# Half of an output product moved from the last stage of a decoder layer into its attention stage

## The chip, the cores and the metric

The kernel runs on one core of one Trainium2 chip. A core has a matmul engine (PE, with a weight load of its own, PEld), a vector engine (DVE), a scalar engine (ACT), GpSimd (POOL) and SyncE (SP), which here issues all the transfers. The metric is the device time of one execution in microseconds (us). Before the change it is 2042.25 us, the median of three runs (2040.35 to 2043.14).

## The reference

One decoder layer for 2048 tokens of width 1024, in f32. Shortened to what matters here:

```python
n = rms_norm(h, norm_g)
dq, dk, dv, dgate, cq, ckv, kr, mgate = jnp.split(n @ w_in, offsets, axis=-1)
# differential attention: 4 heads, 2 softmax maps a head, keys of 64, values of 128, causal
sc = jnp.einsum('bqhmd,bkhmd->mbhqk', rope(dq), rope(dk)) * 64 ** -0.5
pr = softmax(where(mask, sc, -inf))
od = rms_norm((pr[0] - lam * pr[1]) @ dv, subln_g) * (1.0 - lam_init) * silu(dgate)
# latent attention: 8 heads, from low-rank queries, keys and values, causal
om = mla_attention(...) * silu(mgate)
h = h + concatenate([od, om], axis=-1) @ w_out          # 1024 x 1024: rows 0-511 for od, 512-1023 for om
h = h + (p @ w_ple) * sigmoid(h @ w_ple_gate)           # 256 x 1024 and 1024 x 1024
return rms_norm(h, final_norm_g)
```

The output product is a sum over two halves of w_out: the rows that meet the differential heads (od) and those that meet the latent heads (om). The embedding product p @ w_ple depends on inputs alone.

## The kernel before

It works in four stages, one after the other, with tokens in 16 blocks of 128. Every f32 product is made as three matmuls of fp32r operands that are split in a high and a low part (high by high, high by low, low by high), so a product of 1024 by 512 columns is 8 x 3 matmuls of 512 columns.

1. Projections (0 to about 716 us): n @ w_in and what follows from it up to both attentions. Queries, keys and values, the gates (`gate_s`), all go to DRAM. The rotated queries and keys of the differential heads are stored split, in `dq_s`.
2. Latent attention (about 716 to 1162 us), ordered by a planner that is not touched. Its output goes to `zm_s`.
3. Differential attention (about 1162 to 1577 us). `load_head` brings a head's keys, queries and values: for each map one slot of queries (high part on partitions 0 to 63, low part on 64 to 127) and two slots of keys (high part twice, low part twice). The work is written in tasks. `block(h, b)` makes the scores of 128 queries against all earlier keys, in units of up to 1024 keys, for two maps: `unit` has the matmuls (L870, L871), a causal mask added by a matmul (L873) and the maximum on DVE (L874); when all units of a map are there, `expo` makes the negated, scaled maximum (L880 or L882) and the exponential on ACT, with its sum (L885). `combine` weighs the second map by lambda and the quotient of the sums and adds it to the first: on POOL for the first 1024 keys where there are two units (L899, L900), on DVE for the last unit (L902). `weigh(h, g)` takes two blocks: transposes of the probabilities (`tpa`, L930), a copy by ACT (`ah`, L932 or L934), products with the values (`pod`, L942), two transposes at the end (L952), the norm and a store to `zd_s`. `load_out` brings w_out and splits it in 32 pieces, in the last head.
4. Final stage (about 1577 to 2040 us), block by block from the last: `load_mix` loads attention output (1024 wide), gate, x and p, POOL makes gate times output (L807), 8 transposes (`zt4`), the output product p1 (48 matmuls, L1053 to L1055), x added by DVE (L1088), the embedding product p3 (12 matmuls), 8 transposes of the sum (`ht4`), the gate product p2 (48 matmuls), sigmoid, product, sum and norm. Weights for p3 and p2 are loaded and split at its start (L1033 to L1035), those for p3 first. `split_ps` (L110, L111) makes the high part by an ACT copy and the low part by a DVE subtraction.

PSUM holds 8 banks. In the differential stage: three score tiles of two banks each, one bank for transposes (`ps_t`), one for the products with values (`ps_o`).

The order on each engine comes from two things. `merge` deals the tasks of two lists by their costs, `weigh` of one pair of blocks with `block` of the next ones. The order that results is the priority by which a list scheduler of the framework places the instructions; so the order on an engine differs from that of the code. Each engine does its instructions in that order and waits on semaphores for the others.

Of the kernel before, what the change touches and what calls it, by code (L numbers as in the profile page):

```python
# [18 lines left out]
P = 128  # L19
# [6 lines left out]
LAM_INIT = 0.2  # L26
TWO_PI = 6.283185307179586
# [10 lines left out]
WN = 6  # L38
# [5 lines left out]
DROP = 3  # L44
TAIL = 2

# [18 lines left out]
def tile_hymba(ctx, tc, a, out):  # L65
# [19 lines left out]
    zm_s = [scratch(f"zm_s{t}", [512, 512]) for t in range(NT)]  # L85

# [109 lines left out]
    with ExitStack() as c1:  # L196
# [162 lines left out]
        for m in range(2):  # L359
            wg, wn = wn, (load_w(512, 512) if m == 0 else load_w(2560, 272))  # L360
            for t in range(NT):
# [4 lines left out]
                for g in range(4):  # L366
# [8 lines left out]
                    V.tensor_mul(t1, pt, tcos)  # L375
                    for q in range(4):
                        V.tensor_mul(t2[32 * (q ^ 1):32 * (q ^ 1) + 32], pt[32 * q:32 * q + 32],
                                     tsin[32 * q:32 * q + 32])
# [218 lines left out]
    def load_head(h):  # L597

        ts = list(range(NT)) if h % 2 == 0 else list(reversed(range(NT)))
        hd = heads[h] = {}  # L600

        def begin():
            for t in ts:
                tg = dict(tag="vbig", bufs=2) if h % 2 == 1 and t >= 2 else dict(tag="big")
                hd[t] = xpool.tile([P, 7, 512], F32R, name="hd", **tg)

        def one(t, m, i):
            for j in range(2 + i * 2):
                nc.sync.dma_start(out=hd[t][64 * (j % 2):64 * (j % 2) + 64, 3 * m + i + j // 2].bitcast(F32),
                                  in_=dq_s[i][t][j // 2 if i == 1 else j, h, m * 64:(m + 1) * 64, :])  # L610

        def val(t):
            nc.sync.dma_start(out=hd[t][:, 6].bitcast(F32).rearrange("p (j d) -> p j d", d=P),
                              in_=dv_s[t][:, h * P:(h + 1) * P].rearrange("(j p) d -> p j d", p=P))

        tasks = [(0, begin)] + [(0.5, lambda t=t, m=m, i=i: one(t, m, i)) for m in range(2) for i in range(2) for t in ts]
        return tasks + [(0.1, lambda t=t: val(t)) for t in ts]

# [181 lines left out]
    def mix(b, zg, gt):  # L800

        t, o = b // 4, (b % 4) * P
        nc.sync.dma_start(out=zg[:, 0:512], in_=zd_s[b // 2][b % 2 * P:(b % 2 + 1) * P, :])
        nc.sync.dma_start(out=zg[:, 512:1024], in_=zm_s[t][o:o + P, :])
        nc.sync.dma_start(out=gt, in_=gate_s[b])
        for g in range(2):
            G.tensor_mul(zg[:, g * 512:(g + 1) * 512], zg[:, g * 512:(g + 1) * 512], gt[:, g * 512:(g + 1) * 512])  # L807


    SC_D = 64.0 ** -0.5  # L810
    with ExitStack() as c3:
# [12 lines left out]
        def load_out():  # L824

            tasks = []

            def piece(n):
                k, c = n // 4, n % 4
                if n % 8 == 0:  # L830
                    wt[k // 2] = xpool.tile([P, 2, 2, D], F32R, name="wo", tag="big")
                w = wt[k // 2]
                sl = slice(c * 256, (c + 1) * 256)
                ws = sb.tile([P, 256], F32, name="ws", tag="ws", bufs=3)
                nc.sync.dma_start(out=ws, in_=a["w_out"][k * P:(k + 1) * P, sl])
# [3 lines left out]
            return [(0.3, lambda n=n: piece(n)) for n in range(4 * KT)]  # L839
# [3 lines left out]
        ends = []  # L843

        def block(h, b):
# [8 lines left out]
            def unit(m, u):  # L854
                hd = heads[h]
                if m == 0 and u == 0:
                    st["s"] = sm.tile([P, 2, 2], F32, name="ssum", tag="ssum", bufs=4)
                if u == 0:
# [301 lines left out]
```

## Time and profile before

| | before |
|---|---|
| median of the runs (3) | 2042.25 us |
| profiled execution | 2042.74 us |
| its span, first to last instruction | 2040.5 us |
| mean granted clock of PE over the span | 0.982 |
| latent stage, differential stage, final stage | 446, 415, 463.5 us |

The profiled execution's own time is 2.2 us more than its span. A row of stretches gives start, end and length in us, then the busy time of an engine with its number of instructions in brackets, then PE's granted clock (1.00 is full speed), the DMA share and GB/s. A row of operations gives line, engine, operation, output and inputs, shapes and count, then busy us and the mean ns of one, then the engine's idle time just before them and what ended it. A row of the timeline gives start, duration and the same names; the numbers in square brackets are idle time before it.

### The profile page before, as it was taken

What the parts mean: (1) busy time and instruction counts of PE and PEld (TensorE: products, weight loads), DVE (VectorE), ACT (ScalarE), POOL (GpSimd) and SP (SyncE); (2) the same over time, 40 slices, a digit from 0 to 9 for tenths busy, and PEclk for the clock granted to TensorE, in tenths of its full rate; (3) what the DMA queues carried; (4) which work ended last, traced back from release to release, by engine and by line L of the source; (5) the groups of instructions that cost most, each with busy time, mean ns of one, the idle gap of its engine ahead of it and who ended that gap; (6) DMA issues with size and microseconds to landing.
All of it is one profiled execution on the core that took longest, in us unless ns stands there. A gap on an engine that the chain in (4) does not pass through costs nothing.

```text
span 2040.5 us, 28322 instructions
## 1 busy us (share of the span) xinstructions
PE 1930.3 (95%) x9521; PEld 1520.2 (74%) x9521; DVE 1208.1 (59%) x2685; ACT 917.7 (45%) x2089; POOL 634.4 (31%) x528
## 2 busy tenths in 40 slices
PE   7999999999999699999999989899988899999997
PEld 5788878898887477777777667676666677777786
DVE  5253677632446487888888687677876533333322
ACT  4422001122333467777777677677776311111111
POOL 4400345300000166666656335414441201111100
PEclk9999999999998899999999899999998999999999
DMA  5442333322267643514141311530021522222210
GB/s 165 140 147 87 130 127 135 119 86 77 65 211 255 219 127 105 144 55 130 31 118 42 101 35 43 154 112 27 24 83 56 194 90 68 88 88 88 75 47 21
DMA packets 171680, 209.73 MB, mean 103 GB/s; under 512 B 38876, under 2 KB 99180, under 8 KB 171536
## 3 DMA queue, kind: packets, MB, share of 16 engines
q1 hardware_dynamic: 171536, 207.93, 32.6%
q8 instruction: 75, 1.23, 0.3%
q14 instruction: 69, 0.57, 0.1%
HBM read 129.65 MB, written 78.14 MB: 102 GB/s over the span
## 4 chain that ended last, share of the span: by engine, by line
PE 75%; DVE 7%; ACT 7%; DMA 3%; POOL 2%; issue 2%; SPq 1%; ACTq 0%; POOLq 0%; DVEq 0%
PE p L1053 6%; PE p L1055 6%; PE p L1054 6%; PE ps L252 5%; PE ps L251 5%; PE ps L253 5%; PE pod L942 3%; PE pm L171 3%; PE po L704 3%; PE ps L372 3%; PE pst L675 3%; PE ps L370 3%; PE ps L371 3%; PE po L705 3%; PE pst L674 3%; PE pst L673 3%
## 5 line engine op out<-in xcount | busy, mean ns | idle before, releaser
L690 POOL TENSOR_TENSOR acc<-ph,acc 128x512 f32<-128x512 f32 (+3 forms) x208 | 216.6, 1041 | 165.2 <-DVE acc L685 76.2
L251 PE MATMUL ps<-wh,xh 128*128 128x512 f32 (+1 forms) x640 | 229.6, 359 | 9.6 <-DVE wh L240 7.9
L252 PE MATMUL ps<-wl,xh 128*128 128x512 f32 (+1 forms) x640 | 227.6, 356 | 0.5 <-DVE wl L241 0.4
L253 PE MATMUL ps<-wh,xl 128*128 128x512 f32 (+1 forms) x640 | 226.7, 356 | 0.4 <-DVE xl L228 0.3
L678 ACT ACTIVATE ph<-pst 128x512 fp32r<-128x512 f32 (+1 forms) x320 | 170.2, 532 | 114.1 <-PE pst L675 61.6
L695 DVE TENSOR_TENSOR pl<-pst,ph 128x512 fp32r<-128x512 f32 (+1 forms) x320 | 193.3, 607 | 45.7 <-ACT pst L679 42.9
L874 DVE TENSOR_REDUCE mxd<-pu 128x1 f32<-128x1024 f32 (+4 forms) x192 | 173.1, 908 | 61.9 <-PE pu L873 39.0
L885 ACT ACTIVATE pb<-pu,nm 128x1024 f32<-128x1024 f32 (+4 forms) x192 | 165.6, 866 | 39.3 <-DVE nm L880 25.7
L679 ACT ACTIVATE pst<-pst 128x512 f32<-128x512 f32 (+1 forms) x320 | 169.0, 528 | 0.0
L107 POOL TENSOR_TENSOR s<-s,half 128x2 f32<-128x2 f32 (+1 forms) x48 | 32.6, 679 | 425.0 <-DVE s L106 359.6
L870 PE MATMUL pu<-hd 128*128 128x512 f32 (+3 forms) x320 | 139.8, 437 | 20.6 <-ACT pb L885 17.6
L942 PE MATMUL pod<-ah,hd 128*128 128x256 f32 (+1 forms) x576 | 146.5, 379 | 0.5 <-ACT ah L934 0.5
L251 PEld LDWEIGHTS ps<-wh,xh 128*128 128x128 f32 x640 | 121.5, 190 | 30.2 <-ACT sq L223 6.6
L173 DVE TENSOR_REDUCE mx<-pm 128x1 f32<-128x512 f32 x192 | 130.0, 680 | 14.9 <-PE pm L171 14.8
L253 PEld LDWEIGHTS ps<-wh,xl 128*128 128x128 f32 x640 | 121.2, 190 | 20.1 <-DVE xl L228 2.7
L252 PEld LDWEIGHTS ps<-wl,xh 128*128 128x128 f32 x640 | 121.7, 190 | 18.9 <-DVE wl L241 1.8
L1102 DVE TENSOR_TENSOR sg<-p,sg 128x512 f32<-128x512 f32 (+1 forms) x34 | 20.8, 655 | 175.1 <-ACT sg L1101 175.1
L871 PE MATMUL pu<-hd 128*128 128x512 f32 (+3 forms) x320 | 122.6, 390 | 0.0
L704 PE MATMUL po<-ph,vall 128*128 128x512 f32 (+1 forms) x320 | 117.9, 374 | 4.8 <-ACT ph L678 4.5
L673 PE MATMUL pst<-QH,kall 97*128 97x512 f32 (+2 forms) x296 | 119.1, 402 | 0.0
L171 PE MATMUL pm<-kall,QH 96*128 96x512 f32 (+3 forms) x296 | 115.0, 403 | 3.6 <-DVE mx L173 2.5
L705 PE MATMUL po<-pl,vall 128*65 128x512 f32 (+1 forms) x320 | 115.4, 363 | 0.0
(265 smaller groups left out, 4735.1 us busy)
## 6 DMA issues: line engine op xcount, KB each, us to landing
hd<-dq_s SPq DMA_DIRECT2D x192, 128.0 KB
wr<-in_w_in SPq DMA_DIRECT2D x40, 256.0 KB
xr<-in_xT SPq DMA_DIRECT2D x32, 256.0 KB
dq_s<-th SPq DMA_DIRECT2D x32, 256.0 KB
dq_s<-tl SPq DMA_DIRECT2D x32, 256.0 KB
k_s<-stage SPq DMA_DIRECT2D x16, 512.0 KB
q_s<-stage SPq DMA_DIRECT2D x16, 512.0 KB
v_s<-stage SPq DMA_DIRECT2D x16, 512.0 KB
```

Of the source, the lines that this page charges most:

```text
L171: T.matmul(pm[:, :w], lhsT=q, rhs=keys_of(pr, e, c)[0][0:96, :w], start=True, stop=True)
L251: T.matmul(pt[:, :w], lhsT=h, rhs=wh[k][:, :w], start=(k == 0), stop=False)
L252: T.matmul(pt[:, :w], lhsT=h, rhs=wl[k][:, :w], start=False, stop=False)
L253: T.matmul(pt[:, :w], lhsT=l, rhs=wh[k][:, :w], start=False, stop=(k == KT - 1))
L673: T.matmul(pt[:, o:], lhsT=kh[0:97], rhs=qh[0:97, o:], start=True, stop=False)
L678: A.activation(ph[:, o:], pt[:, o:], AF.Exp, scale=SC_M)
L690: eng.tensor_add(self.acc[:, o:], ph[:, o:].bitcast(F32), self.acc[:, o:])
L695: V.tensor_sub(pl[:, o:], pt[:, o:], ph[:, o:].bitcast(F32))
L704: T.matmul(self.po[:, o:], lhsT=vv[:, 0:128], rhs=ph[:, o:], start=(kc == 0), stop=(kc == self.n - 1))
L705: T.matmul(self.po2[:65, o:], lhsT=vv[:, 64:129], rhs=pl[:, o:], start=(kc == 0), stop=False)
L874: V.reduce_max(st["x", m][:, u:u + 1], pu[:, :w], axis=AX.X)
L942: T.matmul(st["po"][:, o:], lhsT=vv, rhs=st[u][:, i, o:], start=(kc == 0), stop=(kc == nk - 1))
```

## The change

- A new task list, `side_work`, in the differential stage: for each block it loads x, the latent output, its half of the gate and p; POOL makes gate times output; four transposes (`tpf`) go to the transpose pool of that stage; ACT and DVE split them; 24 matmuls (`pf<-wm`) make the latent half of the output product, DVE adds x, and the sum goes to DRAM (`h_s`); 12 matmuls (`pf<-wp`) make the embedding product, copied by ACT and stored (`ple_s`). Both use one PSUM bank, `ps_f`. Its weights (`wm`, `wp`) are loaded and split at the start of the stage. The other half of w_out (`wd`) is loaded in the last 15% of the list (`TAIL_D`). `merge(main, fill)` deals it all among the attention's tasks.
- The final stage loads `h_s` and `ple_s`; it makes 4 transposes of the attention output, not 8, 24 matmuls of the output product, not 48, and no embedding product. The embedding weights are no longer loaded there.
- A head's keys are stored once, high part on partitions 0 to 63 and low part on 64 to 127; the queries, which then must be there twice, are loaded in groups of two blocks (`load_dq`) into two slots that take turns. The number of score matmuls is the same.
- The maximum is kept per unit: DVE makes the negated maximum of a unit, for the second unit the smaller of the two, and the exponential follows each unit (`step`, one unit later in priority). `combine` then corrects the first unit by exp of the difference of the two: a small ACT exponential, two small DVE products and one more POOL scaling of 1024 columns (L989) for each block with two units. The factor 1/8 of the scores goes into the queries in the first stage, by a form with a scalar in place of 160 multiplications.
- PSUM of the differential stage: two score tiles (were three), two banks for transposes (was one), one for values, one for `ps_f`.

The core of the diff:

```diff
@@ first stage @@
-                    V.tensor_mul(t1, pt, tcos)
+                    sc = SC_D if m == 0 else 1.0
+                    V.scalar_tensor_tensor(t1, pt, sc, tcos, op0=ALU.mult, op1=ALU.mult)
...
@@ load_head @@
+        def keys(t, i):
+            nc.sync.dma_start(out=hd[t][64 * i:64 * i + 64, 0:2].bitcast(F32),
+                              in_=dq_s[1][t][i, h].rearrange("(m p) s -> p m s", p=64))
...
+    def load_dq(h, g):
+        q, t, o = heads[h]["q", g % 2], g // 2, g % 2 * 256
+        for i in range(2):
+            for r in range(2):
+                nc.sync.dma_start(out=q[64 * r:64 * r + 64, :, i].bitcast(F32),
+                                  in_=dq_s[0][t][i, h, :, o:o + 256].rearrange("(m p) s -> p m s", p=64))
...
@@ differential stage @@
-        ps_s = c3.enter_context(tc.tile_pool(name="p3pss", bufs=3, space=PSUM, reuse_waits="tile"))
-        ps_t = c3.enter_context(tc.tile_pool(name="p3pst", bufs=1, space=PSUM, reuse_waits="tile"))
+        ps_s = c3.enter_context(tc.tile_pool(name="p3pss", bufs=2, space=PSUM, reuse_waits="tile"))
+        ps_t = c3.enter_context(tc.tile_pool(name="p3pst", bufs=2, space=PSUM, reuse_waits="tile"))
         ps_o = c3.enter_context(tc.tile_pool(name="p3pso", bufs=1, space=PSUM, reuse_waits="tile"))
+        ps_f = c3.enter_context(tc.tile_pool(name="p3psf", bufs=1, space=PSUM, reuse_waits="tile"))
...
+        def side_work(wk, wz, b):
...
+            def load():
+                nc.sync.dma_start(out=xr, in_=a["x"][b * P:(b + 1) * P, :])
+                mix(zm, gt, zm_s[b // 4][b % 4 * P:(b % 4 + 1) * P, :], b, 1)
+            def turn():
+                tp = ps_t.tile([P, 4, P], F32, name="tpf", tag="tpa")
+                for k in range(4):
+                    T.transpose(tp[:, k], zm[:, k * P:(k + 1) * P], ident)
+                split_ps(zh, zl, tp)
...
+            def mul(name, xs, kts, c, n0, n1, end):
...
+                if n0 == 0:
+                    box[0] = ps_f.tile([P, 512], F32, name="pf")
+                for n in range(n0, n1):
+                    T.matmul(box[0], lhsT=steps[n][0], rhs=steps[n][1][:, sl], start=(n == 0), stop=(n == len(steps) - 1))
+                if n1 == len(steps):
+                    end(sl)
+            def add(sl):
+                V.tensor_add(xr[:, sl], box[0], xr[:, sl])
+                if sl.start:
+                    nc.sync.dma_start(out=h_s[b], in_=xr)
+            def keep(sl):
+                A.copy(pe[:, sl], box[0])
...
-                V.reduce_max(st["x", m][:, u:u + 1], pu[:, :w], axis=AX.X)
-            def expo(m):
...
+                V.tensor_reduce(nm[:, m, u:u + 1], pu[:, :w], op=ALU.max, axis=AX.X, negate=True)
+                if u == 1:
+                    V.tensor_tensor(nm[:, m, 1:2], nm[:, m, 0:1], nm[:, m, 1:2], op=ALU.min)
+                def expo():
+                    A.activation(st[m][:, u * 1024:u * 1024 + w], pu[:, :w], AF.Exp, bias=nm[:, m, u:u + 1],
+                                 accum_out=st["s"][:, m, u:u + 1])
+                step([(1, expo)] + ([(2, combine)] if (m, u) == (1, nu - 1) else []))
...
+                if nu == 2:
+                    V.tensor_mul(f[:, 1:2], f[:, 1:2], cc)
+                    sl = slice(0, 1024)
+                    for m in range(2):
+                        G.tensor_scalar(st[m][:, sl], st[m][:, sl], scalar1=f[:, m:m + 1], scalar2=0.0, op0=ALU.mult,
+                                        op1=ALU.add)
+                    G.tensor_add(st[0][:, sl], st[0][:, sl], st[1][:, sl])
...
+        fill = [(0.3, f) for f in load_split_w("wm", a["w_out"], 4, 4, dict(tag="vbig", bufs=2))]
+        fill += [(0.3, f) for f in load_split_w("wp", a["w_ple"], 0, 2, {})]
+        fill += [x for b in range(NB) for x in side_work(wk, wz, b)]
+        wd = load_split_w("wd", a["w_out"], 0, 4, dict(tag="big"))
+        rest = sum(c for c, _ in fill) * TAIL_D / (1 - TAIL_D)
+        fill += [(rest / len(wd), f) for f in wd]
+        merge(main, fill)
...
@@ final stage @@
-        load_split(*wl, a["w_ple"], 2)
         load_split(*wg, a["w_gate"], KT)
...
-            product(p1, zh, zl, *wo, KT)
+            product(p1, zh, zl, *wo, 4)
...
-            p3 = ps.tile([P, D], F32, name="p3", tag="p4")
-            product(p3, ph, pl, *wl, 2)
```

On PE, the matmul engine, in the differential stage. `pu` is a score tile, `tpa` a transpose of probabilities, `pod` the product with values; x2 or x4 means so many in a row. Before, in the first head:

```order
L930 MATMUL tpa<-ident,pb 128x128 x4
L942 MATMUL pod<-ah,hd 128x256 x2
L873 LDWEIGHTS ident_b
L873 MATMUL pu<-mask_b,ident_b 128x128
L930 MATMUL tpa<-ident,pb 128x128 x4
L942 MATMUL pod<-ah,hd 128x256 x2
L870 MATMUL pu<-hd 128x512
L871 MATMUL pu<-hd 128x512
```

With the change, also in the first head. `tpf` is the transpose of the latent output, `pf` the side accumulator, `wm` the latent half of w_out:

```order
L1034 MATMUL pod<-ah,hd 128x256 x2
L882 MATMUL tpf<-ident,wk 128x128 x4
L1022 MATMUL tpa<-ident,pb 128x128 x4
L958 MATMUL pu<-hd 128x512
L959 MATMUL pu<-hd 128x512
L958 MATMUL pu<-hd 128x512
L959 MATMUL pu<-hd 128x512
L961 LDWEIGHTS ident_b
L961 MATMUL pu<-mask_b,ident_b 128x128
L899 MATMUL pf<-wm,wz 128x512 x4
L1034 MATMUL pod<-ah,hd 128x256 x2
L1022 MATMUL tpa<-ident,pb 128x128 x4
```

Between the attention's own matmuls, which keep their order, stand transposes and groups of four matmuls of the side work.

On PE in the final stage, at the end of one block's output product. `zg` is the next block's attention output, `xr` this block's sum, `ht4h` the transposed sum's high part, `wl` the embedding weights, `wg` the gate weights. Before:

```order
L1055 MATMUL p_17703<-wo,zt4l 128x512
L1045 MATMUL tp_17756<-ident,zg 128x128 x4
L1045 MATMUL tp_17763<-ident,zg 128x128 x4
L1053 MATMUL p_17770<-wl_16890,ph_17524 128x512
L1054 MATMUL p_17770<-wl_16892,ph_17524 128x512
...
L1054 MATMUL p_17770<-wl_16893,ph_17524 128x512
L1055 MATMUL p_17770<-wl_16891,pl_17525 128x512
L1045 MATMUL tp_17785<-ident,xr_17520 128x128 x4
L1045 MATMUL tp_17792<-ident,xr_17520 128x128 x4
L1053 MATMUL p_17799<-wg,ht4h 128x512
```

With the change:

```order
L1161 MATMUL p_18643<-wd,zt4l 128x512
L1151 MATMUL tp_18672<-ident,zg 128x128 x4
L1151 MATMUL tp_18681<-ident,xr_18514 128x128 x4
L1159 MATMUL p_18695<-wg,ht4h 128x512
L1151 MATMUL tp_18688<-ident,xr_18514 128x128 x4
L1160 MATMUL p_18695<-wg,ht4h 128x512
```

The twelve matmuls of the embedding product are gone from between the output product and the transposes of its sum, and the second four of those transposes stand behind the first matmul of the gate product.

## Rows read from the trace of the kernel before

**Rows 1.** Engines on the page: busy us, share of the span, instructions.

```profile
PE 1930.3 (95%) x9521; PEld 1520.2 (74%) x9521; DVE 1208.1 (59%) x2685; ACT 917.7 (45%) x2089; POOL 634.4 (31%) x528
```

**Rows 2.** Stretches: bounds, length, then PE, PEld, DVE, ACT, POOL, clock, DMA, GB/s.

```profile
1162.00:1577.00 415.00, 368.11 (x1952) 282.09 (x1952) 311.34 (x731) 301.14 (x780) 157.02 (x97) 0.97 0.23 67
716.00:1162.00 446.00, 438.26 (x2185) 322.41 (x2183) 367.80 (x823) 325.59 (x699) 275.86 (x255) 1.00 0.34 93
1650.00:1960.00 310.00, 306.71 (x1392) 246.00 (x1391) 105.13 (x168) 50.58 (x112) 36.28 (x34) 1.00 0.25 81
1240.00:1280.00 40.00, 36.97 (x197) 28.86 (x197) 29.79 (x57) 28.77 (x63) 20.20 (x11) 1.00 0.24 69
1460.00:1540.00 80.00, 64.76 (x333) 49.90 (x334) 63.75 (x123) 55.34 (x140) 37.85 (x21) 0.96 0.21 68
```

**Rows 3.** Timeline of PE in the differential stage.

```profile
1244.82 0.60 PE L930 MATMUL tpa<-ident,pb 128*128 128x128 f32 x4
1245.25 1.03 PE L942 MATMUL pod<-ah,hd 128*128 128x256 f32 x4
1246.12 0.22 PE L873 MATMUL pu<-mask_b,ident_b 128*128 128x128 bf16 x1
```

**Rows 4.** Timeline of PE in the final stage.

```profile
1828.14 0.40 PE L1053 MATMUL p<-wg,ht4h 128*128 128x512 f32 x1
1830.01 0.40 PE L1055 MATMUL p<-wg,ht4l 128*128 128x512 f32 x1
```

**Rows 5.** Score matmuls L870: idle before them until (us, times).

```profile
  ACT pb L885: 51.9, 90
```

**Rows 6.** Transposes L930: idle before them until (us, times).

```profile
  ACT ah L932: 48.4, 74
```

**Rows 7.** Chain that ended last, in the final stage.

```profile
1656.31 0.88 PE tp L1045 x8
1987.79 0.87 PE tp L1045 x8
```

**Rows 8.** Timeline at the final stage's start: SP's issues, a DVE split.

```profile
1584.12 1.75 SPq L1033 DMA_DIRECT2D wr<-in_w_ple  x4
1590.25 2.13 SPq L1033 DMA_DIRECT2D wr<-in_w_gate  x4
...
1616.38 1.35 DVE L1035 TENSOR_TENSOR wg<-wr,wg 128x512 fp32r<-128x512 f32 x2 [3.28 <-ACT wg L1034]
```

**Rows 9.** Operations of ACT: count, busy us and mean ns, idle before.

```profile
L885 ACT ACTIVATE pb<-pu,nm 128x1024 f32<-128x1024 f32 x80 | 89.2, 1116 | 27.8 <-DVE nm L880 25.7 <-DVE nm L882 1.3
L932 ACT COPY ah<-tpa 128x512 f32<-128x512 f32 x112 | 65.2, 582 | 20.6 <-PE tpa L930 17.0 <-PE pu L873 3.2 <-ACT pb L885 0.2
```

**Rows 10.** Timeline in the final stage: the weight load that waits.

```profile
1826.75 0.19 PEld L1053 LDWEIGHTS p<-wg,ht4h 128*128 128x128 f32 x1 [0.53 <-ACT ht4h L110]
```

**Rows 11.** Operations of DVE, same columns as rows 9.

```profile
L874 DVE TENSOR_REDUCE mxd<-pu 128x1 f32<-128x1024 f32 x80 | 97.5, 1219 | 34.9 <-PE pu L871 21.8 <-PE pu L873 12.4
L837 DVE TENSOR_TENSOR wo<-ws,wo 128x256 fp32r<-128x256 f32 x32 | 22.9, 734 | 3.1 <-ACT wo L836 3.1
L1088 DVE TENSOR_TENSOR xr<-p,xr 128x512 f32<-128x512 f32 x32 | 20.6, 686 | 61.7 <-PE p L1055 61.7
L891 DVE TENSOR_TENSOR ssum<-ssum 128x2 f32<-128x2 f32 x32 | 4.9, 154 | 8.7 <-ACT pb L885 8.7
L375 DVE TENSOR_TENSOR t<-ps,tcos 128x512 f32<-128x512 f32 x32 | 22.1, 692 | 52.5 <-PE ps L372 44.5 <-DMA tcos<-tab_s 6.5 <-issue 1.4
L228 DVE SCALAR_TENSOR_TENSOR xl<-xr,norm_g,xh 128x512 fp32r<-128x512 f32 x32 | 27.8, 872 | 44.1 <-ACT xh L220 44.0
```

**Rows 12.** Operations of POOL, same columns.

```profile
L899 POOL TENSOR_SCALAR pb<-pb,cc 128x1024 f32<-128x1024 f32 x32 | 54.2, 1693 | 98.0 <-DVE cc L895 45.3 <-DVE nm L880 33.7 <-ACT wo L836 6.0
L807 POOL TENSOR_TENSOR zg<-zg,gt 128x512 f32<-128x512 f32 x30 | 40.9, 1385 | 142.4 <-PE p L1055 81.0 <-DMA zg<-zd_s 28.4 <-DMA gt<-gate_s 23.8
```

**Rows 13.** DVE subtraction L1072: shortest, median and longest in ns.

```profile
L1072 DVE TENSOR_TENSOR pl<-pr,ph x16: 414/1360/1539, 1581.6 to 1991.6; 128x256 fp32r<-128x256 f32 x16
```

More of the change, by code (lines that the diff above doesn't have):

```diff
@@ L26 @@
 LAM_INIT = 0.2
+SC_D = 0.125
 TWO_PI = 6.283185307179586
@@ L44, with merged @@
 DROP = 3
+TAIL_D = 0.15
 TAIL = 2
+def merged(a, b):
+    out = []
+    merge(*([(x[0], lambda x=x: out.append(x)) for x in y] for y in (a, b)))
+    return out
 def merge(a, b):
@@ L85, in tile_hymba @@
     zm_s = [scratch(f"zm_s{t}", [512, 512]) for t in range(NT)]
+    h_s = [scratch(f"h_s{b}", [P, D]) for b in range(NB)]
+    ple_s = [scratch(f"ple_s{b}", [P, D]) for b in range(NB)]
     const = ctx.enter_context(tc.tile_pool(name="const", bufs=1))
@@ L798, in tile_hymba, with mix, zd_of @@
             tick()
[L800 to L810, printed above, removed]
+    def mix(zg, gt, src, b, c):
+        nc.sync.dma_start(out=zg, in_=src)
+        nc.sync.dma_start(out=gt, in_=gate_s[b][:, c * 512:(c + 1) * 512])
+        G.tensor_mul(zg, zg, gt)
+    def zd_of(b):
+        return zd_s[b // 2][b % 2 * P:(b % 2 + 1) * P, :]
     with ExitStack() as c3:
@@ L822, in tile_hymba, with load_split_w, piece @@
         wt = {}
[L824 to L832, printed above, removed]
+        def load_split_w(name, src, k0, kts, tg):
+            def piece(k, c):
+                if k % 2 == 0 and c == 0 and (name, k // 2) not in wt:
+                    wt[name, k // 2] = xpool.tile([P, 2, 2, D], F32R, name=name, **tg)
+                w = wt[name, k // 2]
@@ L843, in tile_hymba, with step @@
         ends = []
+        def step(new=()):
+            for x in late:
+                x[0] -= 1
+            due = [x for x in late if x[0] <= 0]
+            late[:] = [x for x in late if x[0] > 0] + [list(x) for x in new]
+            for _, f in due:
+                f()
         def block(h, b):
@@ L868, in unit @@
                     o = pu[:, c * 512:c * 512 + cw]
-                    q = hd[t][:, 3 * m, j * P:(j + 1) * P]
-                    T.matmul(o, lhsT=q, rhs=hd[kc][:, 3 * m + 1, :cw], start=True, stop=False)
-                    T.matmul(o, lhsT=q, rhs=hd[kc][:, 3 * m + 2, :cw], start=False, stop=not last)
+                    qh, ql = (hd["q", b // 2 % 2][:, m, i, b % 2 * P:(b % 2 + 1) * P] for i in range(2))
+                    T.matmul(o, lhsT=qh, rhs=hd[kc][:, m, :cw], start=True, stop=False)
@@ L945, in finish @@
             def finish():
+                while ends:
+                    ends.pop(0)()
                 ot = sb.tile([P, 256], F32, name="otd", tag="otd", bufs=1)
@@ L974, in weigh, with finish_late, next_end, last_mix @@
             return tasks
-        order = [(h, g if h % 2 == 0 else NB // 2 - 1 - g) for h in range(4) for g in range(NB // 2)]
+        order = [(h, g) for h in range(4) for g in groups(h)]
         blocks = [(h, 2 * g + j) for h, g in order for j in range(2)]
         LEAD = 3
-        for x in blocks[:LEAD]:
-            merge(block(*x), [])
-        pending, wload = [], load_out()
+        def finish_late():
+            while late:
+                step()
+        def next_end():
+            if ends:
+                ends.pop(0)()
+        def last_mix():
+            box["mixed"] = xpool.tile([P, 2, 512], F32, name="mixed", tag="vbig", bufs=2)
+            mix(box["mixed"][:, 0], box["mixed"][:, 1], zd_of(NB - 1), NB - 1, 0)
+        box = {}
+        main = [x for y in blocks[:LEAD] for x in block(*y)]
+        pending = load_head(1)
+        pending.pop(0)[1]()
+        wt["wp", 0] = xpool.tile([P, 2, 2, D], F32R, name="wp", tag="big")
+        wk = xpool.tile([P, 4096], F32, name="wk", tag="big")
+        wz = pp.tile([P, 1536], F32R, name="wz")
         for i, (h, g) in enumerate(order):
-            if i % 8 == 0 and h < 3:
+            if i % 8 == 0 and 0 < h < 3:
                 pending = load_head(h + 1)
-            if h == 3:
-                pending, wload = pending + wload[:WN], wload[WN:]
             n = -(-len(pending) // max(1, HE - i % 8)) if h < 3 else len(pending)
```

159 lines of the change are left out of this document (81 added, 78 removed).

## The prediction

> **What bounds the kernel now.** I read the page's engine table first: PE, the matmul engine, is busy 1930 of the 2040.5 us [rows 1]. Then the table of stretches, one row for each stage [rows 2]. In the latent stage (716 to 1162 us) PE is busy 438 of 446 us at full clock, in the middle of the final stage (1650 to 1960) 307 of 310. Those two do nothing but what PE needs. In the differential stage (1162 to 1577) it is busy 368 of 415, and DVE, ACT and POOL are further from full than that. So it is the only stage with room on PE, and the room is larger than the busy column says, because a matmul's record is longer than the time until the next may follow. I therefore read the spacing of starts on the timeline. Four transposes take 1245.25 − 1244.82 = 0.43 us, 0.108 each; two value products (each two records of 256 columns) take 1246.12 − 1245.25 = 0.87, 0.435 each [rows 3]. A 512-column matmul takes 0.234: eight intervals from 1828.14 to 1830.01 [rows 4].
>
> At these spacings the differential stage of before needs: scores, counted in the code, 4 heads x 2 maps x 34,816 columns, two passes folded in, 278,528 columns at 0.234 per 512 = 127 us; 288 value products at 0.43 = 124; 606 transposes at 0.108 = 65; 128 mask products at about 0.06, the 0.05 between its start and the next row's being a lower end and its own 0.22 an upper, = 8. That is 324 us of the 415: 91 us in which PE could have done more. The clock explains about 12 of them (mean granted clock 0.97 in this stage [rows 2], 415 x 0.03). Most of the rest is two waits: score matmuls wait 51.9 us until the exponential has freed a score tile [rows 5], transposes wait 48.4 us until ACT has emptied the one transpose tile [rows 6] (these lists count the weight-load queue with the matmul queue, so their sum may be over 91).
>
> **What moves.** Out of the final stage, for each of 16 blocks: 24 of the 48 matmuls of the output product, the 12 of the embedding product, and 4 of 16 transposes. 36 x 0.234 + 4 x 0.108 = 8.86 us a block, 141.8 in all. The same instructions come into the differential stage, so its floor becomes 324 + 142 = 466 us. Moving them gains nothing by itself: it pays only as far as they fall into PE's 91 us.
>
> **Final stage, given back.** In the steady part the chain of waits is PE alone: from the transposes at 1656.31 to those at 1987.79 lie 12 blocks, 27.62 us each, of which 8.86 go [rows 7]. Two things keep the stage from giving all 141.8. First, the gate weights. Now the embedding weights are asked for at 1584.12, the gate weights from 1590.25, and the last piece is split at 1616.38 + 1.35 = 1617.7 [rows 8]; until then PE lives on the output and embedding products of two blocks, some 15 us of which are gone. The gate weights are now first in the queue, 6.1 us earlier, so 15 − 6 = 9 us are lost. Second, the 12 embedding matmuls (2.8 us) stood between the output product and the transposes of its sum; without them ACT has two copies of 0.58 to make [rows 9] before the gate product may start, where before it had one. Such a wait shows already as 0.53 us [rows 10]; I take another 0.5 for about 14 blocks, 6 to 7 us (0 if the next block's work fills it, 16 if both the sum's 0.69 [rows 11] and a copy are uncovered). Sum: −141.8 + 9 + 6 = −127 us.
>
> **Differential stage.** Its other engines first, each new piece priced at its nearest row. DVE: 32 additions at 0.686, 16 splits of the same size, 8 more weight pieces at 0.734, and about 160 operations on one or two columns at 0.154 [rows 11]: 22 + 11 + 6 + 25 = 64, so at most 375 busy us. ACT: 16 + 32 copies at 0.582 [rows 9], 8 weight copies and 32 one-column exponentials, at most that again = 28 + 23: at most 352. POOL: 32 more scalings at 1.693 and 16 products at 1.385 [rows 12], 32 operations of half that size at most 1.385: 54 + 22 + 44 = 120, at most 277. All stay under the 466 of PE and near the proportions of the latent stage, where DVE has 368, ACT 326 and POOL 276 beside a PE busy 438 of 446 [rows 2]. So I expect no other engine to become the bound; POOL's second scaling is hidden as there, and if it were not, it would delay a block's transposes by 1.7 us, 32 times = 54 us.
>
> The waits. A pair of score tiles was freed late, because the exponential of the first 1024 keys had to wait for the maximum of the second: from the last score matmul of the first unit, one more unit of PE work (324 / 192 units = 1.7), a maximum of 1.22, a small operation of 0.15 and the exponential of 1.12 [rows 9, 11] = 4.2 us, while three tiles give PE 3 x 1.7 − 0.94 = 4.1 us of other work. That is the 51.9 us. With a running maximum the tile is free after 1.22 + 0.15 + 1.12 = 2.5 us, and with two tiles, but 466 / 192 = 2.4 us of PE work a unit, the cover is 2 x 2.4 − 0.94 = 3.9. The chain gets 1.4 us of slack where it had none. The second transpose tile takes away most of the 48.4: a tile is copied in 0.58 while the other fills. New is the single accumulator of the side work: its next group waits for DVE's addition or ACT's copy (0.69 or 0.58 and the queue before it), with 0.9 to 1.5 us of other PE work between in the order. There are 64 such groups; I take 0.1 to 0.2 us each, near 10. On SP, which issues the loads in order, come 4 loads and 2 stores for each block of side work, 96 at 1.75/4 = 0.44 us [rows 8], 42 us over the stage; a load of x stands there behind the store of the sum, and a block of side work has some 27 us (506 x 0.85 / 16). Queries come in pieces of 128 KB, two pairs of blocks ahead; the bytes are what they were, DMA share there is 0.23 [rows 2], and I take 0 (2 us for each of 32 groups if a load comes late: 64).
>
> So how dense will PE be? From below, as in the latent stage: 438 / 446, which makes 466 into 475. From above, nothing of the 91 is used: 557. The nearest row is the densest stretch of the present stage, 1240 to 1280, busy 36.97 of 40 = 0.92 [rows 2]; with the two waits loosened I take 0.95, between it and the latent stage. 466 / 0.95 = 491, plus the 12 of the clock, plus 3 after the last fill: 506 us, 91 more than the 415.
>
> **The first stage** turns 160 multiplications of DVE into a form with a scalar: 0.692 now, 0.872 for such a form with operands in memory [rows 11], at most 160 x 0.18 = 29 us of DVE, less where the operand is in PSUM. PE holds that stretch and DVE has idle time there (52.5 us before these very lines). I take 0.
>
> **Sum.** Profiled execution 2042.7 us (span 2040.5 and 2.2 around it), 0.5 above the median of 2042.25: 2042.7 + 91 − 127 = 2007 us.
>
> **DVE beside POOL.** DVE's subtraction of 128x256, both inputs in SBUF, took 0.41 us at best and 1.36 in the median, with POOL's multiplications running beside it [rows 13]: 0.95 more. POOL's share of the stage rises from 157/415 to 277/506, by 0.17. If the 168 DVE operations of that kind (weight pieces, weighted sums, scaled outputs) lose 0.95 us so much more often, DVE is busy 168 x 0.95 x 0.17 = 27 us more, 402 of 506, which doesn't reach PE by itself. The Trainium skill ("SBUF — State Buffer", section "Who interferes with whom") has the rule behind it: DVE and POOL share a port pair, and a DVE instruction with two SBUF inputs blocks against a POOL instruction that reads SBUF. The row agrees with it.
>
> **Rivals.**
> 1. Half of the waits stay (chance 0.15): accumulator, late pieces of queries, and DVE, in order, standing at the running sum until ACT's small exponential is done. For it: each of them is a new wait behind a busy queue. Against: 1.4 us of slack in the score chain. PE's idle then is 64 instead of 40, stage 530: 2042.7 + 115 − 127 = 2031 us.
> 2. DVE's operations stretch beside a POOL that is busy 120 us more, as the 1.36 beside 0.41 [rows 13] shows, and all 27 us reach PE (0.05): 2007 + 27 = 2034 us. Against: DVE has over 100 us free. The Trainium skill's section named above would expect the stretching itself.
> 3. Slower (0.20): two score tiles are too few. The tile chain of 2.5 us stands in queues: on DVE behind an addition, a weight piece or a split (0.69 to 0.73), on ACT behind a copy (0.58). If a tile meets about two of these, 2.5 + 1.4 = 3.9 us, the slack is gone, and side work only pushes the units apart: idle stays 91, stage 557, 2042.7 + 142 − 127 = 2058 us. It decides from 76 us of idle on (stage over 542). For it: 80 us with weight pieces in the queues (1460 to 1540) have PE at 64.8 of 80 [rows 2], and the change puts 40 pieces there. Against: the latent stage, with the same mixture, is dense.
> 4. Denser (0.12): the stage comes near the latent stage, 475 + 12 = 487, or the final stage gives back less: 2042.7 + 72 − 127 = 1988, down to 1975.
>
> **How the numbers follow.** The forecast has chance 0.48, and its own range is 1990 to 2022 (stage 490 to 521). The time can tell 0.2%, 4 us, from no change: 2038 to 2046. Faster: forecast 0.48, rival 4 0.12, rival 2 0.05, rival 1 all but 0.02 = 0.78. Same: that 0.02 and 0.03 of rival 3. Slower 0.17. The range takes in rivals 1, 2 and most of 4 and the lower edge of 3: 1980 to 2046.
>
> **What would show it.** Right: the differential stage 490 to 521 us long, PE's busy share there above 0.95, score matmuls waiting for the exponential well under 51.9 us, transposes for ACT under 20; the final stage 336 us, with steady blocks near 19 us and the first gate product about 6 us earlier. Wrong: PE waiting over 76 us in the differential stage (for the exponential: rival 3; for the side accumulator or queries: rival 1; for DVE operations grown beside POOL: rival 2), or a final stage over 345 us.

## The result: 14 us slower

The changed kernel takes 2056.5 us (median of four runs, 2055.3 to 2059.9) against 2042.7 for the kernel before, measured beside it: a ratio of 1.007, interval 1.0053 to 1.0088, so 0.5 to 0.9% slower. Its profiled execution has a span of 2054.9 us. The forecast of 2007 was wrong in sign; the time is near that of the third rival, 2058.

Stretches of the changed kernel, with the columns of [rows 2]: latent stage, differential stage, final stage, and the differential stage again in its first 60 us, its middle and its last 60 us.

```profile
716.00:1161.00 445.00, 437.49 (x2180) 321.68 (x2178) 366.89 (x823) 325.11 (x697) 275.90 (x255) 1.00 0.31 85
1161.40:1704.20 542.80, 499.57 (x2592) 397.16 (x2593) 378.26 (x819) 337.05 (x867) 226.37 (x176) 0.97 0.40 125
1704.20:2055.00 350.80, 307.71 (x1394) 241.68 (x1392) 129.21 (x219) 79.09 (x172) 28.61 (x32) 0.97 0.32 107
1161.40:1221.40 60.00, 49.41 (x218) 37.17 (x219) 44.63 (x105) 38.84 (x110) 12.93 (x13) 0.82 0.54 162
1221.40:1644.20 422.80, 400.89 (x2105) 320.75 (x2104) 292.87 (x615) 258.93 (x643) 195.54 (x149) 1.00 0.41 130
1644.20:1704.20 60.00, 49.26 (x272) 39.24 (x271) 40.77 (x101) 39.28 (x116) 17.89 (x15) 0.96 0.17 51
```

The differential stage has grown from 415 to 543 us, 128 where 91 were forecast; the final stage has shrunk from 463 to 351, 112 to 113 where 127 were forecast. At the start the differential stage has come 0.7 us earlier, so the first two stages are untouched. With a floor of 466 us, PE's idle time in the differential stage fell from 91 to 77 us, where 40 were expected. In the middle PE is busy 401 of 423 us; the ends are thin, 49 of 60 each, and the first has a mean granted clock of 0.82. Before, the same first 60 us were:

```profile
1162.10:1222.10 60.00, 54.22 (x276) 40.76 (x276) 48.06 (x124) 44.44 (x121) 18.39 (x13) 0.93 0.23 64
```

The two waits that were to shrink did. Idle time before score matmuls, and then before transposes of probabilities (us, times), in the changed kernel; they answer to [rows 5, 6]:

```profile
  ACT pb L968: 33.9, 48
```

```profile
  POOL pb L991: 15.0, 10
...
  ACT ah L1024: 4.4, 4
```

In PE's own waits of this stage (us, times, longest) the exponential still leads, and POOL's weighted sum, which now stands behind a second scaling, has become the second:

```profile
PE pu L958 <- ACT pb L968: 12.5, 18, 2.0
PE tpa L1022 <- POOL pb L991: 7.0, 5, 2.0
PE pf L899 <- DVE wk L904: 5.5, 7, 2.6
```

In the final stage each steady block now has two waits, 1.02 us for DVE's sum and 0.73 us for ACT's copy. The timeline of one block, and the first transposes of the next block's sum:

```profile
1867.72 0.60 PE L1151 MATMUL tp<-ident,zg 128*128 128x128 f32 x4
1869.34 0.66 PE L1151 MATMUL tp<-ident,xr 128*128 128x128 f32 x4 [1.02 <-DVE xr L1189]
1870.73 0.50 PE L1159 MATMUL p<-wg,ht4h 128*128 128x512 f32 x1 [0.73 <-ACT ht4h L121]
```

```profile
1889.69 0.66 PE L1151 MATMUL tp<-ident,xr 128*128 128x128 f32 x4 [1.02 <-DVE xr L1189]
```

1889.69 − 1869.34 = 20.35 us a block, for 72 x 0.234 + 12 x 0.108 = 18.1 of PE work. Before it was 27.62 for 27.0 [rows 7]. So a block gave 7.27 us, not 8.86.

### The profile page after: what moved, and what is told of

Read it like the earlier page. It is cut to its first block, busy times and chain, and to the rows that moved or that the text cites. A ratio compares the mean times of both kernels' runs of the same rounds, so it can differ in the third digit from the quotient of the medians.

```text
span 2054.9 us, 28677 instructions
## 1 busy us (share of the span) xinstructions
PE 1926.3 (94%) x9521; PEld 1521.5 (74%) x9521; DVE 1238.9 (60%) x2721; ACT 944.7 (46%) x2157; POOL 682.4 (33%) x592
## 5 line engine op out<-in xcount | busy, mean ns | idle before, releaser
L963 DVE TENSOR_REDUCE nm<-pu 128x1 f32<-128x1024 f32 (+4 forms) x192 | 173.6, 909 | 88.5 <-PE pu L961 68.5
L958 PE MATMUL pu<-hd 128*128 128x512 f32 (+3 forms) x320 | 133.6, 418 | 14.0 <-ACT pb L968 12.5
L899 PE MATMUL pf<-wm,wz 128*128 128x512 f32 x384 | 118.9, 424 | 7.9 <-DVE wz L122 3.8
L989 POOL TENSOR_SCALAR pb<-pb,f 128x1024 f32<-128x1024 f32 x64 | 87.6, 1369 | 104.6 <-ACT f L978 59.7
L1159 PE MATMUL p<-wg,ht4h 128*128 128x512 f32 (+1 forms) x272 | 107.5, 395 | 14.7 <-ACT ht4h L121 9.9
L1034 PEld LDWEIGHTS pod<-ah,hd 128*128 128x128 f32 x576 | 105.4, 193 | 18.8 <-ACT ah L1024 2.5
```

The costliest lines, as they stand in the source:

```text
L899: T.matmul(box[0], lhsT=steps[n][0], rhs=steps[n][1][:, sl], start=(n == 0), stop=(n == len(steps) - 1))
L963: V.tensor_reduce(nm[:, m, u:u + 1], pu[:, :w], op=ALU.max, axis=AX.X, negate=True)
L1034: T.matmul(st["po"][:, o:], lhsT=vv, rhs=st[u][:, i, o:], start=(kc == 0), stop=(kc == nk - 1))
L1159: T.matmul(pt[:, sl], lhsT=xh_[:, k], rhs=wh[k][:, sl], start=(k == 0), stop=False)
```

## The experiments

The question was where the gain went: the attention with fewer score tiles, the side work, the stage's ends, or the final stage. The kernels without side work, the one without the running maximum and the one before with two tiles have one execution each. As a measure of the scatter: the differential stage, the same in the changed kernel and in the version below that alters only the final stage, took 542.8 and 546.7 us in their traces.

**Attention alone.** The fill list keeps its costs and does nothing until the last weight pieces:

```diff
+        fill = [(c, lambda: None) for c, _ in fill]
```

> The changed kernel without its side work and without the loading of the weights for it; the final stage reads x in place of the two stored products. Left out: the latent half of the output product and the embedding product. The attention of the differential stage is then alone with two score tiles, two transpose tiles and the running maximum. PE needs 324 us there. Theory A (the attention itself is loose now, and PE's idle time of the changed kernel is made at the stage's ends and by the side work): stage 360 to 380 us. Rival C (two score tiles are too few, the attention alone keeps the idle time of 77 to 91 us): stage 400 us or more.

Measured: 1966.2 us, with a stage of 451 us: Rival C. The attention alone is far from loose. Then with three score tiles and one transpose tile, as the PSUM of before:

```diff
-ps_s ... bufs=2     -ps_t ... bufs=2     -ps_f = ...
+ps_s ... bufs=3     +ps_t ... bufs=1     +ps_f = None
```

> As the kernel without side work, but with three score tiles and one transpose tile, as before the change. Theory A: the transposes wait for ACT again, the stage is 5 to 20 us longer than with two and two. Rival C: the third score tile takes away at least 20 us.

Measured: 1932.3 us; the stage is 29 us shorter, Rival C again. And with two tiles again and the 24 weight pieces of the side work loaded, though not used:

```diff
+        fill = [(c, f if i < 24 else lambda: None) for i, (c, f) in enumerate(fill)]
```

> As the kernel without side work, but the 24 weight pieces for it are loaded and split at the start of the differential stage. Theory A (at the start the pieces stand in DVE's and ACT's queues, where the short blocks of attention need them): the first 60 us of the stage lose 8 to 12 us of PE, and the whole stage is longer by that. Rival D (the start is slow by the granted clock and the short blocks alone): under 3 us.

Measured: 1970.8 us. The differential stage of each, with two tiles, with three, and with two and the weights (columns as above):

```profile
1163.00:1614.30 451.30, 378.04 (x1953) 297.08 (x1954) 349.49 (x747) 302.86 (x795) 186.98 (x128) 0.94 0.20 56
```

```profile
1160.30:1582.40 422.10, 367.58 (x1952) 283.54 (x1952) 348.75 (x747) 299.93 (x796) 187.50 (x128) 0.97 0.21 61
```

```profile
1163.00:1617.80 454.80, 379.85 (x1952) 297.27 (x1953) 357.93 (x771) 310.07 (x819) 186.92 (x128) 0.94 0.25 70
```

This splits the 128 us, in the order in which the pieces were put back. The new form of the attention with the old PSUM (and with 16 weight pieces in the last head, not 32): 422 − 415 = 7. Two score tiles and two transpose tiles for three and one: 451 − 422 = 29; no run changes the score tiles alone, and the third one is worth more than 29 if the second transpose tile brings something. The weights: 3.5. The side work itself: 543 − 455 = 88, for 142 us of PE work, so 54 of it are hidden. The 7 and the 3.5 are near the scatter.

The first 60 us without the weights and with them:

```profile
1163.00:1223.00 60.00, 50.72 (x241) 37.41 (x241) 47.93 (x107) 39.89 (x108) 17.18 (x13) 0.87 0.29 84
```

```profile
1163.00:1223.00 60.00, 48.62 (x208) 35.28 (x209) 50.53 (x124) 42.89 (x124) 13.43 (x12) 0.81 0.50 148
```

PE makes 208 matmuls there in place of 241. So the pieces do hold the start up, though by less than the 8 to 12 us of Theory A, and the whole stage by 3.5, which is hardly more than Rival D's 3.

PE's waits without side work, with two tiles and then with three:

```profile
PE pu L958 <- ACT pb L968: 35.9, 42, 3.7
PE tpa L1022 <- POOL pb L991: 21.7, 13, 2.2
```

```profile
PE pu L958 <- ACT pb L968: 15.1, 21, 1.7
PE pzd L1046 <- ACT otd L1041: 12.5, 15, 1.7
PE tpa L1022 <- ACT ah L1024: 10.8, 19, 1.6
PE tpa L1022 <- POOL pb L991: 9.9, 8, 1.9
```

In the kernel before, the same wait was:

```profile
PE pu L870 <- ACT pb L885: 17.6, 31, 1.3
```

With three tiles and a running maximum PE waits for the exponential 15.1 us, against 17.6. So with three tiles the new form as a whole gained nothing (422 us against 415). It holds more than the running maximum (smaller loads of queries, a second scaling on POOL), and these were not tried apart.

**What the running maximum is worth with two tiles.** First in the changed kernel:

```diff
-            for u, m in ((u, m) for u in range(nu) for m in range(2)):
+            for m, u in ((m, u) for m in range(2) for u in range(nu)):
...
+                if u < nu - 1:
+                    step()
+                    return
...
+                    for v in range(nu):    # both exponentials, with the common maximum
```

> The changed kernel with the running maximum undone: both units of a map first, then the maximum, then both exponentials, and one scaling on POOL as before; two score tiles and the side work stay. Theory C (two tiles are short, and the running maximum is what frees them early): in 64 maps with two units PE is held until the exponential of the first unit has ended, about 1.2 + 1.1 us and what stands in the queues, 1 to 2 us each beyond what the side work covers: 60 to 130 us longer than the changed kernel, 2115 to 2190 us. Rival E (the side work covers the wait anyhow, and the extra scaling on POOL costs as much as the running maximum brings): within 15 us of the changed kernel.

Measured: 2079.2 us, 23 more than the changed kernel: between the two theories. Its differential stage:

```profile
1159.70:1724.10 564.40, 511.11 (x2593) 398.78 (x2594) 365.11 (x723) 333.33 (x835) 188.31 (x144) 0.97 0.39 120
```

Then two tiles in the kernel before:

> The kernel before the change, with two score tiles and two transpose tiles instead of three and one: what the exchange in PSUM does to the old attention, without a running maximum and without side work. Theory C (two score tiles are too few): without side work to cover it, in each of 64 maps with two units PE waits for both maxima and the first exponential, 40 to 100 us longer, 2080 to 2140. Rival E (the second transpose tile gives back the 17 us that transposes wait for ACT, and the third score tile did little): within 15 us of 2042.

Measured: 2163.5 us, 123 more than the kernel before, measured beside it. Its differential stage, and PE's waits there:

```profile
1160.40:1700.90 540.50, 418.39 (x1953) 319.46 (x1954) 325.19 (x731) 306.06 (x779) 150.88 (x97) 0.85 0.18 52
```

```profile
PE tpa L930 <- POOL pb L900: 48.9, 20, 5.4
PE pu L870 <- ACT pb L885: 46.9, 46, 2.9
```

So the exchange in PSUM alone costs the old attention 125 us (540 − 415), more than Theory C's 40 to 100. PE's idle time grows by 75 of them, from 415 − 368 to 540 − 418. The other 50 are busy time: the same matmuls take 418 us in place of 368, at a mean granted clock of 0.85 in place of 0.97. The wait of the transposes for POOL's weighted sum, 1.3 us in the kernel before, is as large here as that for the exponential. The new form of the attention brings the 540 to 451, and side work covers much of what is left: with two tiles and no running maximum, the stage is 540 us without the 142 us of side work and 564 with them (between these two kernels the loads and the weight pieces differ too).

**The final stage.** The output product of the next block is put ahead of this block's gate product:

```diff
+            hh, hl = transpose_split(xr, "ht4", 1)
+            if b > 1:
+                z[b - 2] = transpose_split(z[b - 2], "zt4", 2)
+            if b > 0:
+                first(b - 1)        # p1 of the next block and the sum
             p2 = ps.tile([P, D], F32, name="p2", tag="p4")
```

> The changed kernel, with the output product of the final stage made one block ahead, so that 24 matmuls stand between the transposes of a block's sum and its gate product. Theory A (the final stage lost its cover: in each block PE waits 1.0 us for DVE's sum and 0.7 us for ACT's copy, as the trace of the changed kernel shows): steady blocks fall from 20.35 us to about 18.4, some 14 of them, so 2056.5 - 27 = about 2030 us. Rival B (the block is bound by the chain of sigmoid, products and norm or by its loads, and PE's waits only move): steady blocks stay above 19.8 and the time above 2048 us.

Measured: 2024.6 us, ratio to the kernel before 0.9915 (0.9899 to 0.9932), 32 us less than the changed kernel. Two blocks of its timeline:

```profile
1891.29 1.03 PE L1151 MATMUL tp<-ident,xr 128*128 128x128 f32 x8
...
1909.65 1.03 PE L1151 MATMUL tp<-ident,xr 128*128 128x128 f32 x8
```

18.36 us a block, 1.99 less; the final stage is 319 us long. PE's two waits, 14.2 and 9.9 us in the changed kernel, are now:

```profile
PE p L1159 <- ACT ht4h L121: 1.3, 2, 0.8
PE tp L1151 <- DVE xr L1182: 0.3, 1, 0.3
```

Theory A holds: the lost cover was the cause.

**The ends of the stage.** On top of that version:

```diff
-TAIL_D = 0.15
+TAIL_D = 0.05
```

> The kernel with the output product one block ahead, and the pieces of w_out's other half dealt in the last 5% of the side list instead of the last 15%. Theory A (in the last 69 us of the stage PE lacks side work and loses some 11 us): 3 to 8 us faster than that kernel's 2024.6. Rival F (the 16 pieces then stand close together in DVE's and ACT's queues, or the final stage waits for them): the same or up to 10 us slower.

Measured: 2017.9 us, ratio 0.9892 (0.9877 to 0.9907), the fastest of all. The last 60 us of the stage, first in the version with the longer tail, then with the shorter one:

```profile
1647.80:1707.80 60.00, 50.62 (x270) 40.31 (x269) 39.83 (x100) 38.70 (x114) 17.48 (x14) 0.92 0.16 49
```

```profile
1639.30:1699.30 60.00, 52.96 (x294) 42.41 (x293) 36.73 (x92) 38.08 (x110) 16.03 (x15) 0.99 0.27 90
```

The gain over the version without it, 6.7 us, is as Theory A said, though the two intervals overlap.

```diff
-                V.tensor_sub(w[:, k % 2, 1, sl], ws, ...)      # cost of a piece 0.3
+                eng.tensor_sub(w[:, k % 2, 1, sl], ws, ...)    # eng is POOL for wm and wp, cost 0.15
```

> The kernel with the output product one block ahead, with the low part of the 24 weight pieces at the stage's start made by POOL, which is busy 13 of the first 60 us, instead of DVE, and the pieces dealt at half their cost. Theory A (at the start DVE holds PE up, and side work comes 40 us late): side work starts 10 us earlier, 5 to 12 us faster than 2024.6. Rival D (clock and short blocks set the start): within 3 us of it.

Measured: 2032.4 us, 8 more. Neither theory: the first matmul of the side work came 38.9 us after the stage's start in place of 42.4, and the stage was 555 us long in place of 547.

```diff
+        wgs = load_split_w("wg", a["w_gate"], 0, 4, dict(tag="big"))
+        fill = fill[:cut] + merged(fill[cut:], [(0.3, f) for f in wgs])
```

> The kernel with the output product one block ahead, with half of the gate weights loaded and split during the last side blocks of the differential stage, and the list's tail at 10%. Theory A (the first gate product waits for the gate weights until 34 us after the final stage begins, PE idle some 24 us of its first 60): half of that wait goes, 6 to 12 us faster than 2024.6. Rival G (16 more pieces on DVE and ACT hold the attention up as much): within 3 us of it, or slower.

Measured: 2021.8 us, ratio 0.9912, no difference from 0.9915: Rival G. With the shorter tail as well:

> The kernel with the output product one block ahead and the tail at 5%, with half of the gate weights loaded during the last side blocks. Theory A: the final stage is 6 to 10 us shorter (306 in the one without) and the differential stage at most 3 longer, 2010 to 2015 us. Rival G: what the final stage gains, the attention loses to 16 more pieces in its queues: 2016 to 2021 us.

Measured: 2027.3 us, ratio 0.9936 (0.9910 to 0.9961), 9 more than without the early weights and outside both ranges. The stage was 558 us long against 542, in a profiled execution of 2035.2 us, the slowest of the four. The expectation's 306 us for the final stage of the version without them was not right: from 1699.3 to 2015 us it is 316.

```diff
-        return list(range(NB // 2)) if h % 2 == 0 else list(reversed(range(NB // 2)))
+        return list(range(NB // 2)) if h == 2 else list(reversed(range(NB // 2)))
```

> The kernel with the output product one block ahead and the tail at 5%, with the first head's pairs of blocks taken from the longest to the shortest, as in the second and fourth. Theory A (the stage begins with short blocks, in which DVE and ACT have much to do for little PE work, while side work must wait for its weights, so PE idles 22 of the first 60 us): long blocks cover that time, the short ones come when side work is there; idle of the first 60 us under 14, 6 to 14 us faster than 2017.9. Rival D (the clock's fall at the stage's start and the wait for weights set it): within 4 us.

Measured: 2034.4 us, 16 more: Theory A is refuted, and Rival D's 4 us is passed too. Long blocks make the start worse:

```profile
1161.50:1221.50 60.00, 43.38 (x155) 31.88 (x156) 43.36 (x79) 31.65 (x71) 24.93 (x16) 0.70 0.49 140
```

PE is busy 43 of 60 us at a mean granted clock of 0.70, and the side work's first matmul comes 51.8 us after the stage's start, not 41.0. That long blocks without side work stand at the two tiles would explain it, but no run shows this apart from the later side work.

> Output product one block ahead, tail at 5%, half of the gate weights early and the first head reversed. If both edits add up: 2000 to 2009 us; if the first head's order does nothing, the same as the one without it.

Measured: 2040.9 us, 23 more than with the shorter tail alone: the losses of the last two edits, 9 and 16, about add up.

## Why the prediction was wrong

**The step that failed** is the density of the differential stage, the 466 / 0.95 + 12 + 3 = 506 us, and in it the paragraph on waits: it held a cover of 2.4 us of PE work a unit, a mean over the stage, against the chain of each tile. The stage took 543, 37 more. Its three parts are the time before the side work's first matmul, the time of the side work, and the time after its last:

```profile
1161.40:1202.30 40.90, 30.88 (x130) 22.27 (x131) 34.64 (x81) 29.75 (x84) 3.92 (x5) 0.75 0.58 168
1202.30:1634.90 432.60, 410.12 (x2142) 328.21 (x2141) 296.98 (x626) 261.71 (x655) 198.68 (x153) 1.00 0.41 131
1634.90:1704.20 69.30, 58.56 (x323) 46.68 (x322) 46.63 (x114) 45.59 (x130) 23.77 (x19) 0.96 0.19 62
```

At the prediction's spacings (the time from one matmul's start to the next, [rows 3, 4]), the matmuls in these parts come to about 20, 396 and 52 us, so PE loses 21, 37 and 17 us.

- The two ends, 110 us of the stage, lose 38 us. Of the forecast's 40 us some 19 would fall there, with all of the clock's 12 and the last 3 put to them. So about 20 us of the miss are the ends. There the attention is alone, without the cover that the forecast spread over the whole stage, and alone with two tiles it needs 451 us, where its old form had 415 with three. At the start the weight pieces and the clock of 0.75 are added; how the 21 us divide among the three isn't shown.
- With side work beside it, the attention did become looser, as the paragraph said. PE's wait for the exponential, up to 1220 us, from 1220 to 1640, and from there on:

```profile
PE pu L958 <- ACT pb L968: 8.1, 9, 2.0
```

```profile
PE pu L958 <- ACT pb L968: 2.0, 6, 0.5
```

```profile
PE pu L958 <- ACT pb L968: 2.4, 3, 1.2
```

- Even so this part loses 37 us and not 21, about 16 us of the miss. The 0.95 was read from busy shares (0.92 in the densest stretch, 438 of 446 in the latent stage) but divides 466, a sum of spacings, and a busy share is the larger of the two, as a matmul's record is longer than the spacing. The stretch from 1240 to 1280, busy 36.97 of 40, holds some 34.5 us of matmuls at these spacings, 0.86. In the merged part the busy share is 0.95, just as forecast, and the matmuls fill 0.92.

That the side work and its weights add 88 + 3.5 us to the attention alone, and that the forecast had 91 more for the stage, is luck: the forecast hid 51 us in a stage of 415, the runs hid 54 in one of 451.

About a third of the 29 us for the exchange of tiles is busy time: the same matmuls take 378 us at a mean clock of 0.94, and 368 at 0.97. The other 19 are PE's idle time, 73 us in place of 54.

**The explanation of the 51.9 us** isn't borne out. With three tiles and the running maximum the same list still shows:

```profile
  ACT pb L968: 39.6, 56
```

PE's own wait falls only from 17.6 to 15.1. So the late exponential was not what made most of it, as far as this pair of kernels tells. A likely part of what is left lies in the new chain itself, where the small operation was priced at 0.15. The maximum of a map's second unit now takes a DVE operation on two tensors in SBUF (L965), where the kernel before had one on a tensor and a scalar per partition (L880), never over 0.216 us. First the new operation with three tiles, then in the changed kernel with one of its long cases:

```profile
L965 DVE TENSOR_TENSOR nm<-nm x64: 136/159/2327, 1187.4 to 1537.9; 128x1 f32<-128x1 f32 x64
```

```profile
L965 DVE TENSOR_TENSOR nm<-nm x64: 144/160/2339, 1200.4 to 1660.2; 128x1 f32<-128x1 f32 x64
```

```profile
1647.16 2.35 POOL L991 TENSOR_TENSOR pb<-pb 128x1024 f32<-128x1024 f32 x1
1647.46 2.07 DVE L965 TENSOR_TENSOR nm<-nm 128x1 f32<-128x1 f32 x1
1649.56 0.37 ACT L968 ACTIVATE pb<-pu,nm 128x128 f32<-128x128 f32 x1 [0.74 <-DVE nm L965]
```

The three numbers are the shortest, median and longest in ns. 15 of the 64 in the changed kernel and 23 of the 64 with three tiles took more than twice the median, each of them while a POOL operation ran, up to that one's end in the case shown. ACT's exponentials stood 19.4 us for this operation in the changed kernel and 30.1 with three tiles. How much of it reaches PE isn't known; no run changes it.

**The final stage** failed by a size: the cover of the embedding product was priced at 0.5 us a block, with 16 us in all as the upper end, if both the sum and a copy are uncovered. PE's waits in the stage show that both are, 24 us in all:

```profile
PE tp L1151 <- DVE xr L1189: 14.2, 14, 1.7
PE p L1159 <- ACT ht4h L121: 9.9, 14, 0.7
```

A block lost 8.86 − 7.27 = 1.6 us, 14 blocks 22 us instead of 6 to 7: the 15 us by which the stage missed. The experiment that put the next product there took back 32. The gate weights were as forecast: the last piece is split at 1738.59 + 1.32, 35.7 us after the stage's start, where the rows of the forecast give 34.4 (1617.7 − 6.1 − 1577.2).

```profile
1738.59 1.32 DVE L1140 TENSOR_TENSOR wg<-wr,wg 128x512 fp32r<-128x512 f32 x2 [1.72 <-ACT wg L1139]
```

**The third rival** had the time by luck, and the reason in part. Two tiles are too few for the attention alone, by 29 us. But its idle time of 91 with nothing else lost is not what happened: 77 stayed, just past its point of decision (the stage is 543, it decided from 542), and the final stage gave back 15 less; the two misses, 14 and 15, cancel. In the merged kernel PE's wait for the exponential is only 12.5 us, 8.1 of them before side work comes. The waits for the side accumulator itself (L904, and 0.7 us for L909) come to 6.2 us, where near 10 was taken.

**The other engines** came near their bounds or under them: DVE 378 (at most 375 said, so 3 over), ACT 337 (352), POOL 226 (277). POOL's scaling took 1.37 us in the mean instead of 1.69:

```profile
L989 POOL TENSOR_SCALAR pb<-pb,f 128x1024 f32<-128x1024 f32 x64 | 87.6, 1369 | 104.6 <-ACT f L978 59.7 <-DVE f L986 44.8
```

Rival 2 came in part, and not where it was sought. DVE's weight pieces took 0.42 us in the median in both kernels; the 0.73 of [rows 11] is a mean with a few long ones in it, up to 2.59 us. First the pieces of the kernel before, then the first ones of the changed kernel, at a time when POOL is busy only 13 of 60 us:

```profile
L837 DVE TENSOR_TENSOR wo<-ws,wo x32: 405/418/2593, 1462.8 to 1523.1; 128x256 fp32r<-128x256 f32 x32
```

```profile
L859 DVE TENSOR_TENSOR wm<-ws,wm 128x256 fp32r<-128x256 f32 x16 | 6.3, 419 | 0.3
```

What did stretch are the small operations of the running maximum (L965 above, 0.357 us in the mean where 0.154 was taken). Queries in small pieces cost nothing that the waits show, and the first stage is hidden, as taken.

Open: three score tiles together with the side work weren't tried, because the side accumulator needs the bank. So how much of the merged stage's 77 us is due to the missing tile isn't known, only that the exchange costs 29 without side work.

## What to carry to other kernels

When work is moved into a stage with idle time, price first what the room for it (here a score tile) costs that stage by itself, and only then how much of the moved work hides. Work that leaves a stage leaves its waits uncovered; look at what stood behind each moved instruction, and put the next block's independent work in its place. When a floor is added up from spacings, take the density from spacings too, and price each stretch by the work that is there, not by the mean. With that one reordering and a shorter tail the same change is 1.1% faster than the kernel before. The reordering was not tried on the kernel before; its blocks, 27.62 us for 27.0 of PE work, would give at most 0.6 us each, an estimate of 9 us in all.

## What the hardware showed unexpectedly

In these runs PE's waits went with a lower granted clock, and so cost more than their own length. The attention's matmuls are the same in number. With three tiles PE idled 54 us and was busy 368, at a mean clock of 0.97; with two it idled 73 and was busy 378, at 0.94; in the old attention with two it idled 122 and was busy 418, at 0.85. The lowest was 0.70, in the first 60 us of the reversed order.

A DVE operation on a single column with both inputs in SBUF, 0.16 us in the median, took up to 2.34 us while POOL worked. It stands in the chain that frees a score tile, and ACT's exponentials waited 19.4 us for it in the changed kernel.
